# Experts' tokens gathered as rows from rows split in two float32r parts, then transposed; the experts' weight ring of ten slots in three places

## The chip, the cores and the metric

The kernel runs on one core of one Trainium2 chip. The metric is the device time of one execution in microseconds (us), the median of the runs shown. TensorE multiplies and transposes, VectorE and ScalarE work on rows and move results out of the accumulators (PSUM), GpSimd does small arithmetic on SBUF, and SyncE's queue starts nearly all the loads.

## The reference

Two networks run one after the other on 512 tokens of 1024 numbers, in float32. Only the end of the first matters here, a layer of 16 experts in which each expert picks its 64 best tokens:

```
aff = softmax(h @ w_router)                  # 512 x 16
g, idx = top_k(aff transposed, 64)           # each of 16 experts picks 64 tokens
xs = h[idx]                                  # 16 x 64 x 1024
y = (silu(xs @ w_gate) * (xs @ w_up)) @ w_down * g
out = sum of y at the tokens that it came from
```

h is the normalised row times (1 + scale) plus shift. After this layer the first network's final norm follows, and then the second network, whose first part is a feed-forward layer.

## The kernel before, in words

Everything is written with a tile framework: pools of tiles in SBUF and PSUM, instructions in program order, and a scheduler that puts them in order on each engine's queue by their readiness in its own model. The order on each queue is fixed when the kernel is built.

All weights come through one object, W. Its pieces (chunks of up to 1 MB, 128 partitions x 2048 numbers) are loaded in the order in which they are used, by SyncE's queue, into slots of a ring. Before the experts' stage the ring has NR = 4 slots (ring 0). For the experts a second ring of NR2 = 5 slots (ring 1) is opened, and piece number n goes to ring 0 if n mod 9 is under 4, otherwise to ring 1, so that both together are a ring of nine. A slot is used again when the matmuls that read it are done. The second network's weights go through ring 0 alone.

Experts are worked on in pairs, q = 0 to 7, 64 tokens each, so 128 columns. A pair has 24 pieces: 8 each of gate, up and down. The stage is this loop:

```
xs, hx = gather(0), None
for q in range(NE // 2 + 1):
    if q < NE // 2:
        outs = gate_up(xs)
        if q + 1 < NE // 2:
            xs = gather(q + 1)
    if q > 0:
        done = down(q - 1, hx)
    if q < NE // 2:
        hx = hidden(q, outs)
    if q > 0:
        scatter(*done)
```

So the gather of the next pair stands beside gate and up of this one, and one turn of the loop is called a round below. A gather makes a one-hot matrix oh (token rows x 128 slots) on VectorE (L855), and multiplies the normalised rows h2f with it so that the result has features as rows, 128 slots as columns (L864): 2 groups x 4 blocks x 4 row tiles, in float32, of which the profile shows two instructions for each matmul. VectorE applies scale and shift on the way to xs (L867, L868). The expert matmuls are in both() at L885, in float32, the two experts of a pair side by side in 64 columns each. hidden() transposes the hidden rows (L906) and copies them (L907); scatter() is at L932 and L934.

h2f comes from normed(t) at L744, ScalarE, for each of four row tiles, during the projection before the stage. The xs tiles use, one after the other, the two large tiles bigh and bigl (16 KB a partition each), which hold matrix operands before and after this stage. The stage begins with the ranking of the tokens on VectorE (L821, L822), for which an exponential (L792) and a transpose come first; the first gather follows it. After the loop come the final norm, the norm of the second network (L277) and its first weights, which are split in two float32r parts, whi on ScalarE (L156) and wlo on VectorE (L157). float32r is float32 read at reduced precision by TensorE; a number split into a rounded part and the rest needs a matmul for each part.

Of the kernel before, what the change touches and what calls it, by code (L numbers as in the profile page):

```python
# [9 lines left out]
F32 = mybir.dt.float32  # L10
F32R = mybir.dt.float32r
BF = mybir.dt.bfloat16
I32 = mybir.dt.int32
AF = mybir.ActivationFunctionType
OP = mybir.AluOpType
# [3 lines left out]
P = 128  # L19
D = 1024  # L20
S = 512
T = S // P
K = D // P
# [6 lines left out]
CAP = 64  # L30
# [16 lines left out]
MAGIC = 12582912.0  # L47

NR = 4
NR2 = 5  # L50
NU = 4
BANDW = 640
RW = "tile"
# [41 lines left out]
def f(ap):  # L95
    return ap.bitcast(F32)


class Weights:
# [25 lines left out]
    def pump(self):  # L125
        while self.dma_at < len(self.chunks):
            srcs, shape, ring = self.chunks[self.dma_at]
            if not self.room.get(ring):
                return
            self.room[ring] -= 1  # L130
            n = int(np.prod(shape[1:]))
            t = self.pools[ring].tile([P, 2048], F32, name="wraw", tag="wraw")
            v = t[:, :n]
            if len(shape) == 3:
                v = v.rearrange("p (a b) -> p a b", b=shape[2])
            for p0, p1, ap in srcs:
                self.nc.sync.dma_start(out=v[p0:p1], in_=ap)
            self.tiles[self.dma_at] = v
            self.dma_at += 1
# [46 lines left out]
def tile_net(ctx, tc, I, out):  # L186
    nc = tc.nc
    V, A, PE, G = nc.vector, nc.scalar, nc.tensor, nc.gpsimd
# [3 lines left out]
    big = ctx.enter_context(tc.tile_pool(name="big", bufs=2))  # L192
# [9 lines left out]
    W = Weights(nc, raw, NR)  # L202

    def psA():
        return psh[0].tile([P, 1024], F32, name="pA", tag="pA")

    def psB():
        return psh[0].tile([P, 512], F32, name="pB", tag="pB")

    def psC():  # L210
        return psh[0].tile([P, 512], F32, name="pC", tag="pC")
# [3 lines left out]
    def psBC():  # L215
        turn[0] ^= 1
        return psB() if turn[0] else psC()

    cst = const.tile([P, C_KEEP], F32, name="cst")
    X = const.tile([P, T, D], F32, name="X")  # L220
# [9 lines left out]
    ident = cst[:, C_ID:C_ID + P]  # L230
# [112 lines left out]
    for k0 in (4, 6, 0, 2):  # L343
# [5 lines left out]
        c = W.chunk(srcs, (P, 2, D))  # L349
# [9 lines left out]
                W.unit(c, lambda v, u=u: v[:, u:u + 1])  # L359

    nth = [0]

    def plan_pair(w, q):

        for c0 in range(0, D, 256):
            for e in (2 * q, 2 * q + 1):
                c = W.chunk([(0, P, w[e][c0:c0 + 256].rearrange("(p j) n -> p (j n)", j=2))], (P, 2048),
                            ring=int(nth[0] % (NR + NR2) >= NR))
                nth[0] += 1
                W.unit(c, lambda v: v.rearrange("p (j n) -> p j n", j=2), raw=2)  # L370

    for q in range(NE // 2 + 1):
        if q < NE // 2:
            plan_pair(wg, q)
            plan_pair(wu, q)
        if q > 0:
            plan_pair(wd, q - 1)
# [16 lines left out]
    c = W.chunk([(0, P, I["pool_w_2"][0].rearrange("g (k p) n -> p (g k) n", p=P))], (P, 8, 256))  # L394
# [39 lines left out]
    qpool = rowp.enter_context(tc.tile_pool(name="rowp", reuse_waits=RW, bufs=1, side="right"))  # L434
# [60 lines left out]
    for s in range(2):  # L495
# [5 lines left out]
                        in_=I["w_router"][0].rearrange("(c p j) n -> p c (j n)", p=P, j=2))  # L501
# [47 lines left out]
    for b in range(6):  # L549
        xs, t = nxt  # L550
# [7 lines left out]
    for b0 in (0, 2, 4):  # L558
# [11 lines left out]
        for s in range(2):  # L570
            p = psBC()
            for b in range(2):
                for g in range(KV):
# [3 lines left out]
                                             in_=p.rearrange("p (g t) -> p g t", g=KV))  # L577
# [4 lines left out]
    for u in range(4):  # L582
        w = W.next()
        for kk in range(2):
            k = u * 2 + kk
# [3 lines left out]
    for t in range(T):  # L589
# [5 lines left out]
        for g in range(2):  # L595
            p = psA()
# [35 lines left out]
    def twos(row):  # L632

        return row.rearrange("r (c p j) -> r c j p", p=P, j=2)
# [87 lines left out]
        values(n, g, *cur)  # L722


    h2f = qpool.tile([P, T, D], F32, name="h2f", tag="q")
    h2f = [h2f[:, t] for t in range(T)]
    for t in range(T):
        nc.gpsimd.dma_start(out=X[:, t], in_=x_in[t * P:(t + 1) * P])
    accs = []
    for t in range(T):  # L730
        if t < 2:
            a = psA()
# [8 lines left out]
    rs = []  # L741

    def normed(t):
        A.activation(h2f[t], X[:, t], AF.Copy, scale=rs[t])  # L744

    lgp, xts = [], []
    lgs = att.tile([P, T, NE], F32, name="lgs", bufs=1)
# [26 lines left out]
    for t in range(T):  # L774
        for j in range(3):
            z = K - 3 + j
            project_out(t, z, order[z], ws[j])
        for dh in range(2):
            tmp = att.tile([P, 512], F32, name="tmp", tag=("PTh", "PTl")[dh], bufs=2)
            c_ = slice(dh * 512, (dh + 1) * 512)  # L780
            V.tensor_mul(tmp, accs[2 * t + dh], gt1[:, c_])
            (G if dh and t + 1 < T else V).tensor_tensor(out=X[:, t, c_], in0=X[:, t, c_], in1=tmp, op=OP.add)
        if t > 0:
            turned_x(t - 1)
        rs.append(row_rstd(att, X[:, t], D))
        if t > 0:
            logits(t - 1)
            normed(t - 1)
    turned_x(T - 1)
    logits(T - 1)  # L790
    V.tensor_sub(aff, lgs, mx[:, :, None].to_broadcast([P, T, NE]))
    A.activation(aff, aff, AF.Exp)  # L792
    normed(T - 1)
    V.reduce_sum(mx, aff, axis=AX.X)
    V.reciprocal(mx, mx)
# [8 lines left out]
    moe = ExitStack()  # L804
    W.open_ring(1, moe.enter_context(tc.tile_pool(name="raw2", reuse_waits=RW, bufs=NR2)), NR2)
    mp = moe.enter_context(tc.tile_pool(name="moep", reuse_waits=RW, bufs=1))
    slot = mp.tile([P, T, NE], F32, name="slot")
    slotT = mp.tile([NE, S], F32R, name="slotT")
    gcol = mp.tile([P, NE // 2], F32, name="gcol")
    pick = mp.tile([NE, NE // 2, P], F32R, name="pick")  # L810
    V.tensor_copy(pick.rearrange("n q (e c) -> n (q e) c", c=64), ident[:NE, :NE, None].to_broadcast([NE, NE, 64]))
    st = ExitStack()
    rp = st.enter_context(tc.tile_pool(name="rp", reuse_waits=RW, bufs=1))
    p = psB()
# [9 lines left out]
    p = psC()  # L824
# [9 lines left out]
    p = psB()  # L834
# [7 lines left out]
    p = psC()  # L842
# [5 lines left out]
    ex = moe.enter_context(tc.tile_pool(name="ex", reuse_waits=RW, bufs=2))  # L848
    iota = cst[:, C_IOTA:C_IOTA + 64]

    def gather(q):

        oh = ex.tile([P, T, 2, CAP], F32, name="oh", tag="oh", bufs=1)
        for t in range(T):
            V.tensor_tensor(oh[:, t], iota[:, None, :].to_broadcast([P, 2, CAP]),  # L855
                            slot[:, t, 2 * q:2 * q + 2, None].to_broadcast([P, 2, CAP]), op=OP.is_equal)
        ohf = oh.rearrange("p t e c -> p t (e c)")
        xs = big.tile([P, K * S], F32, name="xs", tag=("bigh", "bigl")[q % 2], bufs=1)[:, :K * P]
        xs = xs.rearrange("p (k c) -> p k c", k=K)
        for g in range(2):  # L860
            p = psC()
            for a in range(4):
                for t in range(T):
                    PE.matmul(p[:, a * P:(a + 1) * P], twos(h2f[t])[:, 2 * g + a // 2, a % 2], ohf[:, t],  # L864
                              start=t == 0, stop=t == T - 1)
            k_ = slice(4 * g, 4 * g + 4)
            V.tensor_mul(xs[:, k_], p.rearrange("p (k c) -> p k c", k=4), sc2[:, k_, None].to_broadcast([P, 4, P]))  # L867
            V.tensor_add(xs[:, k_], xs[:, k_], sh2[:, k_, None].to_broadcast([P, 4, P]))  # L868
        pg = psC()
        for t in range(T):  # L870
            PE.matmul(pg[:, 0:NE], ohf[:, t], aff[:, t], start=t == 0, stop=t == T - 1)
        for j in range(2):
            V.tensor_copy(gcol[j * 64:j * 64 + 64, q:q + 1], pg[j * 64:j * 64 + 64, 2 * q + j:2 * q + j + 1])
        return xs
# [52 lines left out]
    def scatter(Se, ys):  # L927
        for t in range(T):
            for dh in range(2):
# [4 lines left out]
                V.tensor_add(X[:, t, c_], p, X[:, t, c_])  # L934
# [13 lines that stand above are left out]
# [495 lines left out]
```

## Time and profile before

| | |
|---|---|
| median of 3 runs | 2734.22 us (2734.2 to 2737.8) |
| profiled execution, its own time | 2732.16 us |
| its span in the trace | 2730.0 us |
| mean granted TensorE clock | 0.983 of full speed |
| TensorE matmul busy | 2599.0 us, 95% |
| VectorE, ScalarE, GpSimd busy | 39%, 27%, 3% |
| bytes loaded | 411.94 MB, mean 151 GB/s |

The span is what lies between the first and the last instruction of the profiled execution. Busy times of matmuls are modelled at their ends, so neighbouring matmuls overlap in the rows; the distance between starts says what one costs in a row of them. A DMA share of 1.00 means that all 16 DMA engines were busy.

### The profile page before, as it was taken

To read this page: it belongs to the slowest core of one execution; us is meant where nothing else is said; L and a number is where in the kernel's file an instruction comes from. 1 tells how busy PE (TensorE), PEld (TensorE's weight loads), DVE (VectorE), ACT (ScalarE), POOL (GpSimd) and SP (SyncE) were. 2 spreads that over 40 slices of the span, in tenths; PEclk is the share of its full clock that TensorE was granted. 3 is DMA by queue.
4 is the path that set the end of the run, shared out by engine and by line. 5 is a ranking of instruction groups with operands and counts; after the bars stand their busy time and mean duration, and the time that the engine had idled before them with its cause. 6 is when DMAs were issued, how large, how long until landed. Compare 5 with 4: busy or idle time off the path is not lost.

```text
span 2730.0 us, 29692 instructions
## 1 busy us (share of the span) xinstructions
PE 2599.0 (95%) x12362; PEld 1908.7 (70%) x12362; DVE 1067.1 (39%) x1661; ACT 734.1 (27%) x1268; POOL 78.9 (3%) x138
## 2 busy tenths in 40 slices
PE   5988979999999899999999999999999999999999
PEld 3864755444443688887877777887878777788887
DVE  4646441222221533335533334333334566533332
ACT  4324310000000422223322223222223555422221
POOL 1000000000000100000000000000001100000000
PEclk8989979999999899999999999999999999999999
DMA  8226139999999422322222332322222212122321
GB/s 298 66 105 215 55 159 394 384 389 394 390 392 407 159 95 76 116 89 92 84 102 75 103 100 84 107 95 85 85 92 69 66 57 78 62 93 77 101 89 58
DMA packets 179254, 411.94 MB, mean 151 GB/s; under 512 B 7364, under 2 KB 120544, under 8 KB 151472
## 3 DMA queue, kind: packets, MB, share of 16 engines
q1 hardware_dynamic: 176928, 403.73, 40.5%
q0 software_dynamic: 1184, 2.97, 0.4%
q10 hardware_dynamic: 1008, 3.34, 0.3%
q8 instruction: 97, 1.59, 0.2%
q14 instruction: 37, 0.30, 0.0%
HBM read 407.92 MB, written 2.10 MB: 150 GB/s over the span
## 4 chain that ended last, share of the span: by engine, by line
PE 59%; issue 29%; DVE 3%; ACT 3%; DMA 3%; POOL 1%; ACTq 0%; POOLq 0%; DVEq 0%
PE pA L885 9%; PE pA L242 7%; PE pA L243 7%; PE pA L244 7%; PE pB L885 4%; PE pC L864 3%; PE pC L243 2%; PE pC L242 2%; PE pC L244 2%; PE pB L244 2%; PE pB L243 2%; PE pB L242 2%; DMA wraw<-in_w_ada_dram 1%; PE ms L1314 1%; PE pC L932 1%
## 5 line engine op out<-in xcount | busy, mean ns | idle before, releaser
L156 ACT CAST whi<-wraw 128x1024 fp32r<-128x1024 f32 (+2 forms) x334 | 336.2, 1011 | 1108.1 <-PE pA L243 681.9
L243 PE MATMUL pA<-xTl,whi 128*128 128x512 f32 (+1 forms) x1536 | 578.6, 377 | 1.6 <-DVE xTl L251 1.6
L157 DVE TENSOR_TENSOR wlo<-wraw,whi 128x1024 fp32r<-128x1024 f32 (+2 forms) x334 | 392.2, 1177 | 480.6 <-ACT whi L156 473.2
L244 PE MATMUL pA<-xTh,wlo 128*128 128x512 f32 (+1 forms) x1536 | 578.5, 377 | 0.0
L242 PE MATMUL pA<-xTh,whi 128*128 128x512 f32 (+1 forms) x1536 | 574.8, 382 | 1.7 <-ACT xTh L250 1.3
L242 PEld LDWEIGHTS pA<-xTh,whi 128*128 128x128 f32 x1536 | 290.1, 189 | 77.4 <-ACT sl L969 22.1
L244 PEld LDWEIGHTS pA<-xTh,wlo 128*128 128x128 f32 x1536 | 290.3, 189 | 56.7
L243 PEld LDWEIGHTS pA<-xTl,whi 128*128 128x128 f32 x1536 | 290.4, 189 | 55.3 <-DVE xTl L251 2.1
L885 PE MATMUL pA<-wraw,xs 128*64 128x512 f32 x1024 | 256.7, 598 | 1.5 <-DMA wraw<-in_w_up_dram 1.3
L971 DVE TENSOR_TENSOR sl<-pA,sl 128x512 f32<-128x512 f32 x88 | 60.8, 691 | 427.4 <-PE pA L244 427.3
L885 PEld LDWEIGHTS pA<-wraw,xs 128*64 128x64 f32 x1024 | 73.9, 136 | 136.5 <-issue 128.7
L243 PE MATMUL pC<-wlo,hh 128*128 128x512 f32 x352 | 138.5, 393 | 0.0
L244 PE MATMUL pC<-whi,hl 128*128 128x512 f32 x352 | 138.5, 393 | 0.0
L242 PE MATMUL pC<-whi,hh 128*128 128x512 f32 x352 | 138.4, 393 | 0.0
L242 PE MATMUL pB<-whi,hh 128*128 128x512 f32 x352 | 138.3, 393 | 0.0
L243 PE MATMUL pB<-wlo,hh 128*128 128x512 f32 x352 | 138.3, 393 | 0.0
L244 PE MATMUL pB<-whi,hl 128*128 128x512 f32 x352 | 138.1, 392 | 0.0
L885 PE MATMUL pB<-wraw,hx 128*64 128x512 f32 x512 | 130.7, 596 | 1.6 <-DMA wraw<-in_w_down_dram 1.6
L885 PEld LDWEIGHTS pB<-wraw,hx 128*64 128x64 f32 x512 | 45.9, 136 | 73.3 <-issue 67.2
L864 PEld LDWEIGHTS pC<-oh,h2f 128*128 128x128 f32 x512 | 65.3, 202 | 30.1 <-issue 29.2
L242 PEld LDWEIGHTS pB<-whi,hh 128*128 128x128 f32 x352 | 66.1, 188 | 15.6 <-DVE X L1020 0.7
L244 PEld LDWEIGHTS pB<-whi,hl 128*128 128x128 f32 x352 | 66.1, 188 | 14.9
(474 smaller groups left out, 3201.3 us busy)
## 6 DMA issues: line engine op xcount, KB each, us to landing
wraw<-in_w_gate_dram SPq DMA_DIRECT2D x64, 1024.0 KB, 11.7
wraw<-in_w_up_dram SPq DMA_DIRECT2D x64, 1024.0 KB, 9.0
wraw<-in_w_down_dram SPq DMA_DIRECT2D x64, 1024.0 KB, 7.7
wraw<-in_ffn_w_gate_dram SPq DMA_DIRECT2D x40, 1024.0 KB, 5.2
wraw<-in_ffn_w_up_dram SPq DMA_DIRECT2D x40, 1024.0 KB, 5.2
wraw<-in_ffn_w_down_dram SPq DMA_DIRECT2D x32, 1024.0 KB, 5.0
wraw<-in_w_ada_dram SPq DMA_DIRECT2D x24, 1024.0 KB, 9.5
wraw<-in_ffn_w_down_dram SPq DMA_DIRECT2D x16, 768.0 KB, 4.4
```

The lines of the kernel that those rows point to most:

```text
L156: self.nc.scalar.copy(out=hi, in_=src)
L157: self.nc.vector.tensor_sub(lo, src, f(hi))
L242: PE.matmul(o, a[0], b[0], start=first, stop=False)
L243: PE.matmul(o, a[0], b[1], start=False, stop=False)
L244: PE.matmul(o, a[1], b[0], start=False, stop=last)
L864: PE.matmul(p[:, a * P:(a + 1) * P], twos(h2f[t])[:, 2 * g + a // 2, a % 2], ohf[:, t], start=t == 0, stop=t == T - 1)
L885: PE.matmul(outs[dh][r], x[:, k, r], ws[e][:, j, dh * 512:(dh + 1) * 512], start=k == 0, stop=k == K - 1)
L932: PE.matmul(p, Se[:, t * P:(t + 1) * P], ys[dh][s], start=s == 0, stop=s == 1)
L971: V.tensor_mul(sl, a[:, 512:1024], sl)
L1314: PE.matmul(p[:, :nn], q[a][:, c_], k[b][:, :nn], start=first, stop=False)
```

## The change

The gather is turned round. The normalised rows are kept in two float32r parts: h2h, the rounded row, written by normed(), and h2l, the rest, made after the projection by a ScalarE copy of the normalised row into a tile "got" and a GpSimd subtraction, for each of four row tiles. A gather now multiplies the one-hot matrix, now float32r, from the left: 128 slots as rows, 512 features as columns, two halves, four row tiles, two parts, 16 matmuls. ScalarE copies each half to got (one buffer), and eight transposes bring it to features as rows. Scale and shift follow on VectorE as before.

The ring for the experts has ten slots in three places: ring 0 with four, ring 1 with three, and ring 2 with three, which lie in the two large tiles bigh and bigl, now one tile "wide" each for the whole stage. Both xs buffers lie in the first half of the first of them.

```diff
 NR = 4
-NR2 = 5
+NR2 = 3
+NR3 = 3
...
-            t = self.pools[ring].tile([P, 2048], F32, name="wraw", tag="wraw")
+            if isinstance(self.pools[ring], list):
+                t = self.pools[ring].pop(0)
+                self.pools[ring].append(t)
+            else:
+                t = self.pools[ring].tile([P, 2048], F32, name="wraw", tag="wraw")
...
+    NRS = NR + NR2 + NR3
...
-                            ring=int(nth[0] % (NR + NR2) >= NR))
+                            ring=(NR <= nth[0] % NRS) + (NR + NR2 <= nth[0] % NRS))
...
-    h2f = qpool.tile([P, T, D], F32, name="h2f", tag="q")
-    h2f = [h2f[:, t] for t in range(T)]
+    h2h = qpool.tile([P, T, D], F32R, name="h2h", tag="q")
...
     def normed(t):
-        A.activation(h2f[t], X[:, t], AF.Copy, scale=rs[t])
+        A.activation(h2h[:, t], X[:, t], AF.Copy, scale=rs[t])
...
+    h2l = mp.tile([P, T, D], F32R, name="h2l")
+    for t in range(T):
+        got = mp.tile([P, D], F32, name="got", tag="got")
+        A.activation(got, X[:, t], AF.Copy, scale=rs[t])
+        G.tensor_tensor(out=h2l[:, t], in0=got, in1=f(h2h[:, t]), op=OP.subtract)
+
+    wide = [big.tile([P, K * S], F32, name="wide" + z, tag="big" + z, bufs=1) for z in "hl"]
+    xsb = [wide[0][:, z * D:(z + 1) * D].rearrange("p (k c) -> p k c", k=K) for z in range(2)]
+    W.open_ring(2, [wide[0][:, 2048:4096], wide[1][:, 0:2048], wide[1][:, 2048:4096]], NR3)
...
-        oh = ex.tile([P, T, 2, CAP], F32, name="oh", tag="oh", bufs=1)
+        oh = ex.tile([P, T, 2, CAP], F32R, name="oh", tag="oh", bufs=1)
...
-        ohf = oh.rearrange("p t e c -> p t (e c)")
-        xs = big.tile([P, K * S], F32, name="xs", tag=("bigh", "bigl")[q % 2], bufs=1)[:, :K * P]
-        xs = xs.rearrange("p (k c) -> p k c", k=K)
+        ohr = oh.rearrange("p t e c -> p t (e c)")
+        ohf = f(ohr)
+        got = mp.tile([P, D], F32, name="got", tag="got")
+        for dh in range(2):
+            c_ = slice(dh * 512, (dh + 1) * 512)
+            p = psC()
+            for t in range(T):
+                for z, h in enumerate((h2h, h2l)):
+                    PE.matmul(p, ohr[:, t], h[:, t, c_], start=t + z == 0, stop=t + z == T)
+            A.copy(out=got[:, c_], in_=p)
+        xs = xsb[q % 2]
         for g in range(2):
             p = psC()
             for a in range(4):
-                for t in range(T):
-                    PE.matmul(p[:, a * P:(a + 1) * P], twos(h2f[t])[:, 2 * g + a // 2, a % 2], ohf[:, t],
-                              start=t == 0, stop=t == T - 1)
+                PE.transpose(p[:, a * P:(a + 1) * P], twos(got)[:, 2 * g + a // 2, a % 2], ident)
```

## Rows read from the trace of the kernel before

**Rows 1.** The page: engines' busy time, and load rate in 40 equal slices.

```profile
PE 2599.0 (95%) x12362; PEld 1908.7 (70%) x12362; DVE 1067.1 (39%) x1661; ACT 734.1 (27%) x1268; POOL 78.9 (3%) x138
...
GB/s 298 66 105 215 55 159 394 384 389 394 390 392 407 159 95 76 116 89 92 84 102 75 103 100 84 107 95 85 85 92 69 66 57 78 62 93 77 101 89 58
```

**Rows 2.** Windows by stage: length, engines' busy us, PE clock, DMA share, GB/s.

```profile
391.00:820.00 429.00, 422.92 (x1956) 185.70 (x1957) 93.49 (x172) 19.13 (x33) 0.00 (x0) 1.00 0.95 387
820.00:892.00 72.00, 67.63 (x272) 23.49 (x272) 13.56 (x21) 3.49 (x6) 0.00 (x0) 1.00 0.96 393
```

**Rows 3.** Windows by round, one of five that are alike.

```profile
498.20:562.90 64.70, 63.69 (x291) 27.65 (x289) 14.55 (x26) 2.91 (x5) 0.00 (x0) 1.00 0.94 383
```

**Rows 4.** Windows of 10 us: the stage's first, and one inside a round.

```profile
390.00:400.00 10.00, 10.00 (x54) 4.17 (x54) 2.50 (x8) 0.00 (x0) 0.00 (x0) 1.00 0.41 153
...
540.00:550.00 10.00, 10.00 (x50) 4.06 (x48) 0.00 (x0) 0.00 (x0) 0.00 (x0) 1.00 1.01 419
```

**Rows 5.** Issues of loads; what ended idle time before L885 (us, times).

```profile
wraw<-in_w_gate_dram SPq DMA_DIRECT2D x64, 1024.0 KB, 11.7
...
  DMA wraw<-in_w_down_dram: 6.2, 8
```

**Rows 6.** One gather in a round: the chain (start, us), then the timeline.

```profile
498.27 1.38 PE pC L864 x10
...
504.90 2.55 PE pC L864 x20
...
512.70 2.79 PE pC L864 x22
...
503.16 0.74 PE L864 MATMUL pC<-oh,h2f 128*128 128x128 f32 x4
503.83 1.07 PE L885 MATMUL pA<-wraw,xs 128*64 128x512 f32 x2
```

**Rows 7.** Nearest operations: timeline, first and last of 50; the chain; line groups.

```profile
319.63 0.39 PE L242 MATMUL pC<-whi,mixTh 128*128 128x512 f32 x1
...
330.84 0.39 PE L243 MATMUL pA<-wlo,mixTh 128*128 128x512 f32 x1
...
472.36 1.16 PE pC L906 x8
...
L907 ACT COPY hx<-pC 128x512 f32<-128x512 f32 x8 | 4.7, 586 | 152.8 <-PE pC L906 128.2 <-issue 24.5
```

**Rows 8.** Timeline of the way into the stage, all engines (start, us).

```profile
344.44 1.66 POOL L782 TENSOR_TENSOR X<-X,tmp 128x512 f32<-128x512 f32 x1 [4.38 <-DVE tmp L781]
...
354.90 1.15 ACT L744 ACTIVATE h2f<-X,rstd 128x1024 f32<-128x1024 f32 x1 [0.47 <-POOL rstd L258]
...
363.07 0.26 ACT L792 ACTIVATE aff<-aff 128x64 f32<-128x64 f32 x1 [7.02 <-DVE aff L791]
...
380.75 9.65 PE L864 MATMUL pC<-oh,h2f 128*128 128x128 f32 x64
...
387.39 0.69 DVE L868 TENSOR_TENSOR xs<-xs,sh 128x512 f32<-128x512 f32 x1
...
391.13 4.08 PE L885 MATMUL pA<-wraw,xs 128*64 128x512 f32 x18
...
391.59 0.69 DVE L868 TENSOR_TENSOR xs<-xs,sh 128x512 f32<-128x512 f32 x1
```

**Rows 9.** The way out: timelines of SyncE's queue and VectorE; GpSimd's powers.

```profile
868.34 0.38 SPq L137 DMA_DIRECT2D wraw<-in_ffn_w_gate_dram  x1
888.00 0.38 SPq L137 DMA_DIRECT2D wraw<-in_ffn_w_up_dram  x1
...
900.48 1.21 DVE L157 TENSOR_TENSOR wlo<-wraw,whi 128x1024 fp32r<-128x1024 f32 x1
901.62 1.28 DVE L277 SCALAR_TENSOR_TENSOR hrow<-X,rstd,gain 128x1024 f32<-128x1024 f32 x1
...
L258 POOL TENSOR_TENSOR rstd<-ms,mhalf x8: 548/548/1469, 896.4 to 921.0; 128x1 f32<-128x1 f32 x8
```

## The prediction

> **What bounds the kernel now.** I read the page first: TensorE is busy for 95% of the span, and one stretch of it is also the stretch of highest load rate, the slices at 384 to 407 GB/s [rows 1]. That stretch is the experts' stage, the only place that the diff touches, so the rest of the span was left alone. The windows by stage put the experts' body at 391 to 820 us and its tail at 820 to 892 us [rows 2]. In the body TensorE is busy for 422.9 of 429 us, while the loads run at 387 GB/s. One window per pair of experts then shows what a round is: 64.7 us, PE busy 63.7 of it, DMA share 0.94, 383 GB/s; there are five such rounds, alike within 0.1 us and 10 GB/s [rows 3].
>
> Which of the two is the bound? A stretch inside a round shows the loads at 419 GB/s with a share of 1.01 and PE at 10.00 of 10 us [rows 4]. So the loads can go faster than the round's mean beside a full TensorE. A round loads 24 pieces of 1024 KB, 25.17 MB [rows 5]; at 419 GB/s that is 60.1 us. The round of 64.7 us is thus TensorE's, and the loads sit 4.6 us below it. In the tail, where nothing is gathered, it is the other way round: the expert matmuls' idle time before a weight load has 6.2 us that end with the landing of a piece of the down weights [rows 5]. The reader is to see two limits 7% apart: what is taken from TensorE counts until the loads are reached.
>
> The Trainium skill, page "DMA: Bandwidth & Descriptors", section "Where 436 GB/s comes from", says that for HBM to SBUF transfers the HBM side binds, at about 358 GB/s. By that a round could not be shorter than 25.17 / 0.358 = 70.3 us, an estimate from the page, and the change could win nothing. This trace disagrees: whole rounds run at 383 GB/s, and stretches at 419 [rows 3, 4].
>
> **The change, part by part.** *Gather on TensorE.* Now a gather is 64 matrix instructions at L864. In a regular round the chain shows 52 of them in three pieces of 1.38, 2.55 and 2.79 us; the other 12 stand in three pieces of 4, each 503.83 - 503.16 = 0.67 us [rows 6]. Together 8.73 us. After the change there are 16 float32r matmuls 512 columns wide (2 halves x 4 row tiles x 2 parts) and 8 transposes. Float32r matmuls of that width stand in a row before this stage, 50 of them from 319.63 to 330.84, so 0.229 us each [rows 7]: 3.66 us. Eight transposes of the same shape, those of the hidden rows, take 1.16 us [rows 7]. Together 4.82 us, so 3.9 us less in each round. Seven gathers lie inside rounds (1 to 7): -27.3 us. A round would be 60.8 us, still just above the loads' 60.1.
>
> *Hand-offs that are new.* Each gather now goes matmul, ScalarE copy, transpose, VectorE, where it went matmul, VectorE. Two copies of 128x512 at 0.59 us [rows 7] stand between. ScalarE is nearly idle there, and the gate matmuls that now stand among the gather's pieces can run meanwhile. If they all do, the cost is nothing; if both copies stand bare in PE's queue with about 0.7 us more each for the hand-overs, it is 2.6 us a round. The order of PE's queue after the change is not to be read from this trace; it now mixes gather and gate finely [rows 6], so I take 0.5 us a round, +3.5 us, bounds 0 and +18.
>
> *Low parts of the rows.* Four ScalarE copies (1.15 us, as the one at L744) and four GpSimd subtractions of 128x1024; a GpSimd addition of half that size takes 1.66 us [rows 8], so 3.3 us each. With the single buffer "got" they alternate: 4 x 4.45 = 17.8 us. The last high part is ready at 354.90 + 1.15 = 356.05, and the first gather matmul is at 380.75 [rows 8]: 24.7 us of room, held open by the ranking of tokens on VectorE, so I cost it at nothing. With that cover gone it would be the whole 17.8 us. Behind the copies on ScalarE's queue is the exponential at 363.07 [rows 8], with which the ranking begins: if a copy that waits for GpSimd is put before it, the ranking starts up to one subtraction, 3.3 us, later for each copy ahead.
>
> For the subtractions there is a rule against this change: the Trainium skill, page "SBUF — State Buffer", section "SBUF: two separate sides", says that a VectorE operation with two SBUF inputs and a GpSimd operation that reads SBUF block each other for a whole instruction. The trace agrees: among eight equal GpSimd powers of 0.548 us one took 1.469 us [rows 9], and it ran beside the VectorE step at 901.62, which has two such inputs. By the rule a ranking whose steps had two inputs would wait for the subtractions, 13 us; its steps have one large input, the tensor work.
>
> *First gather.* It stands bare: 10.4 us from the first gather matmul at 380.75 to the first gate matmul at 391.13 [rows 8], the clock being low at first (64 instructions in 9.65 us here against 8.73). Afterwards: 8 matmuls at half speed 3.7, 8 partly so 2.7, copy with hand-over 0.8, the first four transposes 0.6, two VectorE steps of 0.69 us [rows 8] 1.4: 9.2 us, so -1 us (0 to -3).
>
> *Ring of ten.* One more piece, 2.5 us of loading at 419 GB/s, is in place when the rounds start, and the queue can run one piece further ahead. This counts where TensorE waits for loads, in the tail: -2 us (0 to -2.5).
>
> *Which slots the next network finds.* With nine slots, piece 191 is the third in its turn, and only one of the four slots of the first ring is free before the last experts: the first load of the next network goes at 868.34, the second only at 888.00 [rows 9]. With ten, 191 is the second in its turn, so two slots are free and the second load goes some 20 us earlier. What it holds up today is the split at 900.48 on VectorE, ahead of the normalised row at 901.62 [rows 9]: -1 us (0 to -3).
>
> The xs buffers move into one tile, still two of them, so no wait is added there. DMA issues stay the same in number and order.
>
> **The sum.** -27.3 + 3.5 - 1 - 2 - 1 = -27.8 us, against the profiled execution's own 2732.2 us: 2704.4. Its median stands 2.0 us higher, at 2734.2, so 2706 us against that. The loads give a floor of their own: in the body they move 387 x 429 = 166.0 MB, 396 us at 419 GB/s, so 33 us are idle; in the first 10 us, before the first refill, the share is 0.41 [rows 4], so 6 of these stay. That leaves 27 us, 2.5 for the tenth piece, 3 and 3 for start and end at their best: -36 us, 2698. So the two limits nearly coincide, and TensorE's stalls, not its sum, decide the size.
>
> **The rivals.** *Bare hand-offs.* The copies and the ScalarE queue cost all they can: +18 instead of +3.5, and up to 3 at the ranking: about 2722. For it: at the scatter PE waits for ScalarE and VectorE in every round, which is what fills the 1.0 us that a round's PE is not busy [rows 3]. Against it: gate matmuls of another bank are there to fill.
>
> *The loads are the bound already.* If the round's 383 GB/s were all that the loads give in the long run, 24 pieces would take 65.7 us, the round itself, and the time would stay at 2732 to 2734, or 2731 with the tenth piece. The skill's rule above points there. Against it: 419 GB/s over ten microseconds beside a busy PE [rows 4].
>
> *The low parts come late.* The subtractions and the ranking hold each other: +13 us, 2719. Against it: the room of 24.7 us; the ranking reads one tensor at a time.
>
> *Slower: loads into the wide tiles wait for readers of the other parts.* Three slots of the ring and both xs now share two tiles. If a load into one part waited for matmuls that read another, one load per ten would wait for up to a gate-and-up block, 128 x 4.08 / 18 = 29 us [rows 8], with every later load behind it on the one queue, while the ring covers 25 us. At half a block for each of eight rounds that is +116 us, less the 28: about 2820. It decides from 3.5 us of such waiting in a round on. Against it: today the gate matmuls start at 391.13 while the other half of the same xs tile is still being written at 391.59 [rows 8], so parts of a tile are told apart.
>
> **How the numbers follow.** Forecast 0.62, around 2706 (2698 to 2713). Bare hand-offs 0.15, late low parts 0.08, both inside the range's upper part; loads already the bound 0.06; slower 0.07; 0.02 for a gain beyond the floor. The range of 2698 to 2722 leaves out 0.15 to 0.2. What a measurement of this kernel can tell from no change is about 0.2%, 5.5 us. Faster: 0.62 + 0.15 + 0.08 + 0.02 = 0.87; same 0.06; slower 0.07.
>
> **What would show it.** Right: rounds of 60 to 61.5 us at 409 GB/s or more; a gather of 16 + 8 instructions in about 4.8 us; a DMA share near 1.00; the first gate matmul near 390; the next network's second load before 870. Wrong: rounds over 63 us with PE idle behind a copy; gather matmuls that wait for GpSimd; a load into a wide tile that waits while its own slot's readers are done.

## The result, and the profile after

The changed kernel takes 2702.31 us (median of 4 runs, 2700.42 to 2703.63) against 2734.21 us: a ratio of 0.9881, interval 0.9869 to 0.9893. Its profiled execution took 2703.63 us with a span of 2701.6 us, 28.4 us less than the span before.

The page answers [rows 1]: matmul busy time is 30 us less, and the stage's slices now show 414 to 419 GB/s.

```profile
PE 2568.8 (95%) x12042; PEld 1879.9 (70%) x12042; DVE 1066.7 (39%) x1661; ACT 748.4 (28%) x1288; POOL 88.5 (3%) x142
...
GB/s 301 67 86 221 71 164 419 414 418 418 416 417 342 124 94 90 105 86 102 74 94 90 106 86 86 108 80 102 78 101 73 63 57 63 63 94 78 108 83 59
```

The windows by stage and by round answer [rows 2, 3]. The body's DMA share went from 0.95 to 1.00. A round is 60.36 us instead of 64.70, at 417 GB/s; five are alike within 0.05 us.

```profile
391.00:820.00 429.00, 421.05 (x1794) 166.34 (x1791) 94.07 (x169) 28.45 (x49) 0.00 (x0) 1.00 1.00 414
820.00:862.00 42.00, 39.01 (x145) 13.84 (x144) 10.72 (x17) 2.44 (x4) 0.00 (x0) 1.00 0.97 386
539.77:600.13 60.36, 59.35 (x250) 23.60 (x250) 14.59 (x28) 4.08 (x7) 0.00 (x0) 1.00 1.01 417
```

The chain through one round's gather answers [rows 6] (start, us, what). The gather proper stands in five pieces, L879 and L885, from one start to the next 1.36 + 0.67 + 2.51 + 0.68 + 0.43 = 5.65 us (5.54 by the starts in the timeline, where the last is 0.34). Between them two groups of 16 expert matmul instructions are cut into 14 and 2.

```profile
489.62 1.35 PE pC L879 x5
490.98 3.58 PE pA L905 x14
494.55 0.66 PE pC L879 x2
495.22 1.00 PE pA L905 x2
496.22 2.28 PE pC L879 x9
498.50 0.23 PE pC L885 x2
498.73 3.58 PE pA L905 x14
502.31 0.68 PE pC L885 x4
502.99 1.00 PE pA L905 x2
503.99 0.43 PE pC L885 x2
504.42 0.80 PE pC L891 x8
```

The way into the stage answers [rows 8]. The low parts begin on ScalarE at 363.68, behind the exponential, not at 356; the last subtraction ends at 378.09. From the first gather matmul to the first gate matmul it is 388.91 - 381.06 = 7.85 us instead of 10.4.

```profile
363.68 1.13 ACT L819 ACTIVATE got<-X,rstd 128x1024 f32<-128x1024 f32 x1
...
364.89 2.40 POOL L820 TENSOR_TENSOR h2l<-got,h2h 128x1024 fp32r<-128x1024 f32 x1 [8.77 <-ACT got L819]
...
375.75 2.34 POOL L820 TENSOR_TENSOR h2l<-got,h2h 128x1024 fp32r<-128x1024 f32 x1 [1.26 <-ACT got L819]
...
378.27 0.41 DVE L837 TENSOR_SCALAR work<-work 16x512 f32<-16x512 f32 x1
...
381.06 0.77 PE L879 MATMUL pC<-h2h,oh 128*128 128x512 f32 x1
...
388.91 0.65 PE L905 MATMUL pA<-wraw,wideh 128*64 128x512 f32 x2 [0.48 <-DVE wideh L888]
```

The way out answers [rows 9], first SyncE's queue, then VectorE. The row yt, the last result of the last down matmuls, stood at 890.58 before and stands at 860.36 now: 30.2 us earlier. The next network's second load goes at 839.48 instead of 888.00. From yt to the first normalised row, hrow, it is 11.03 us, and it was 11.04. What follows the last yt, code that the change does not touch, took 2701.6 - 860.36 = 1841.2 us, and 2730.0 - 890.58 = 1839.4 before; over all the runs below it lies between 1837.7 and 1843.0. So the stage gained 30.2 us and the span 28.4, and whole times scatter by some microseconds for reasons outside the stage.

```profile
839.48 11.46 SPq L142 DMA_DIRECT2D wraw<-in_ffn_w_up_dram  x1
```

```profile
860.36 1.61 DVE L940 SCALAR_TENSOR_TENSOR yt<-pB,gcol,gt 128x512 f32<-128x512 f32 x2 [8.83 <-PE pB L905]
...
870.26 1.22 DVE L162 TENSOR_TENSOR wlo<-wraw,whi 128x1024 fp32r<-128x1024 f32 x1
871.39 1.28 DVE L282 SCALAR_TENSOR_TENSOR hrow<-X,rstd,gain 128x1024 f32<-128x1024 f32 x1
```

### The profile page after: what moved, and what is told of

Same layout as the page of the kernel before. It is cut to its first block, busy times and chain, and to the rows that moved or that the text cites. A ratio compares the mean times of both kernels' runs of the same rounds, so it can differ in the third digit from the quotient of the medians.

```text
span 2701.6 us, 29081 instructions
## 1 busy us (share of the span) xinstructions
PE 2568.8 (95%) x12042; PEld 1879.9 (70%) x12042; DVE 1066.7 (39%) x1661; ACT 748.4 (28%) x1288; POOL 88.5 (3%) x142
## 4 chain that ended last, share of the span: by engine, by line
PE 58%; issue 30%; DVE 4%; ACT 3%; DMA 3%; POOL 1%; ACTq 0%; POOLq 0%; DVEq 0%; SPq 0%
PE pA L905 8%; PE pA L247 7%; PE pA L248 7%; PE pA L249 7%; PE pB L905 4%; PE pC L248 2%; PE pC L247 2%; PE pC L249 2%; PE pB L249 2%; PE pB L247 2%; PE pB L248 2%; DMA wraw<-in_w_ada_dram 1%; PE pC L879 1%; PE pC L952 1%; PE ms L1334 1%
## 5 line engine op out<-in xcount | busy, mean ns | idle before, releaser
L905 PE MATMUL pA<-wraw,wideh 128*64 128x512 f32 x736 | 202.6, 598 | 1.9 <-DMA wraw<-in_w_up_dram 1.4
L905 PEld LDWEIGHTS pA<-wraw,wideh 128*64 128x64 f32 x736 | 58.3, 136 | 93.2 <-issue 88.2
L905 PE MATMUL pB<-wraw,hx 128*64 128x512 f32 x344 | 101.0, 597 | 1.1 <-DMA wraw<-in_w_down_dram 1.1
L247 PEld LDWEIGHTS pC<-whi,hh 128*128 128x128 f32 x352 | 66.1, 188 | 15.0
L248 PEld LDWEIGHTS pB<-wlo,hh 128*128 128x128 f32 x352 | 66.1, 188 | 14.8
## 6 DMA issues: line engine op xcount, KB each, us to landing
wraw<-in_w_gate_dram SPq DMA_DIRECT2D x47, 1024.0 KB, 13.3
```

Source lines behind the costliest of these rows:

```text
L247: PE.matmul(o, a[0], b[0], start=first, stop=False)
L248: PE.matmul(o, a[0], b[1], start=False, stop=False)
L905: PE.matmul(outs[dh][r], x[:, k, r], ws[e][:, j, dh * 512:(dh + 1) * 512], start=k == 0, stop=k == K - 1)
```

## The experiments

Each time is a median beside a run of the kernel before on the same chip. Two points of the traces serve as a ruler: the first refill (the first load that SyncE's queue issues in the stage, when the first slot comes free), and the last yt. Between them 192 pieces less the ring's must be loaded: 183 with nine slots, 182 with ten, 181 with eleven. At the 420 GB/s that the best whole rounds show, a piece is 1.0486 MB / 420 GB/s = 2.497 us. The last column is what the stage takes from the first refill to the last yt beyond that. "Round" is the median distance of the yt rows of neighbouring rounds. The two points before, and the first of them after (the second stands above):

```profile
394.81 10.63 SPq L137 DMA_DIRECT2D wraw<-in_w_up_dram  x7
890.58 1.61 DVE L920 SCALAR_TENSOR_TENSOR yt<-pB,gcol,gt 128x512 f32<-128x512 f32 x2 [8.83 <-PE pB L885]
```

```profile
392.59 7.69 SPq L142 DMA_DIRECT2D wraw<-in_w_up_dram  x6
```

| kernel | time, us | ratio, interval | round | first refill | last yt | beyond the loads |
|---|---|---|---|---|---|---|
| before, ring of 9 | 2734.21 | 1 | 64.71 | 394.81 | 890.58 | 38.8 |
| old gather, ring of 10 | 2728.91 | 0.9982 [0.9973, 0.9991] | 64.71 | 394.82 | 887.96 | 38.7 |
| old gather in one block, 9 | 2720.66 | 0.9951 [0.9939, 0.9964] | 61.18 | 402.12 | 874.84 | 15.8 |
| new gather, ring of 9 | 2707.02 | 0.9899 [0.9886, 0.9913] | 60.34 | 393.23 | 863.60 | 13.4 |
| changed kernel, 10 | 2702.31 | 0.9881 [0.9869, 0.9893] | 60.33 | 392.59 | 860.36 | 13.3 |
| changed, ring of 11 | 2701.24 | 0.9884 [0.9870, 0.9897] | 60.34 | 392.78 | 858.38 | 13.6 |
| low parts added twice, 10 | 2723.00 | 0.9963 [0.9950, 0.9975] | 63.65 | 395.21 | 881.60 | 31.9 |
| high parts only, 10 | 2697.68 | 0.9866 [0.9851, 0.9881] | 59.84 | 393.79 | 858.89 | 10.6 |
| low parts made twice, 10 | 2708.07 | 0.9909 [0.9894, 0.9925] | 60.34 | 398.87 | 866.05 | 12.7 |
| half the bytes loaded, 10 | 2665.09 | 0.9751 [0.9738, 0.9765] | 56.24 | 390.04 | 825.07 | |
| new gather in one block, 10 | 2705.74 | 0.9901 [0.9884, 0.9917] | 59.84 | 397.79 | 863.33 | 11.1 |
| the same, 11 | 2702.25 | 0.9887 [0.9872, 0.9902] | 59.93 | 398.01 | 860.96 | 11.0 |
| in one block from the third gather, 10 | 2702.45 | 0.9879 [0.9865, 0.9894] | 59.84 | 393.04 | 858.84 | 11.3 |
| the same, 11 | 2700.34 | 0.9876 [0.9859, 0.9892] | 59.84 | 392.62 | 855.94 | 11.4 |

**The two halves of the change apart.** The new gather with a ring of nine:

```diff
-NR3 = 3
+NR3 = 2
-    W.open_ring(2, [wide[0][:, 2048:4096], wide[1][:, 0:2048], wide[1][:, 2048:4096]], NR3)
+    W.open_ring(2, [wide[0][:, 2048:4096], wide[1][:, 0:2048]], NR3)
```

> The gather stays turned round, the ring has nine slots again (ring 2 has two). If TensorE sets the rounds and the loads lie just under it, the tenth slot matters at the two ends alone: one load of 2.5 us less is in place at the start, and the queue runs out a little more often; following the pieces one by one through the slots at 2.5 us a load gives +3 to +5 us against the changed kernel, rounds of 60.4 us as they are. Rival (the ten slots carry the gain): +15 us or more, rounds back over 62 us.

And the old gather with the ring of ten in three places:

```diff
-NR2 = 5
+NR2 = 3
+NR3 = 3
...
-        xs = big.tile([P, K * S], F32, name="xs", tag=("bigh", "bigl")[q % 2], bufs=1)[:, :K * P]
-        xs = xs.rearrange("p (k c) -> p k c", k=K)
+        xs = xsb[q % 2]
```

> The gather of before (64 float32 instructions, 8.7 us), the ring of ten in three places. If the gather carries the gain: rounds stay at 64.7 us, and only the tenth slot's 2.5 us of loading counts, -2 to -3 us against the kernel before, 2731. Rival (the ten slots carry the gain): -15 us or more.

In the stage both came out as expected. From refill to yt the four corners are 495.77 (old, nine), 493.14 (old, ten), 470.37 (new, nine) and 467.77 (new, ten): the ring is worth 2.6 us with either gather, the gather 25.4 us with either ring, and 1.6 to 2.2 us more before the refill. Nothing is left for an interaction. In whole times the new gather with nine slots is 4.7 us above the changed kernel (3 to 5 expected), and the old gather with ten is 5.6 us under its kernel before, where 2 to 3 were expected; the stage shows 2.6 of these, the rest does not come from it.

**More and less work in the gather.** The low parts of the rows left out of the gather, and the low parts added twice:

```diff
-                for z, h in enumerate((h2h, h2l)):
-                    PE.matmul(p, ohr[:, t], h[:, t, c_], start=t + z == 0, stop=t + z == T)
+                PE.matmul(p, ohr[:, t], h2h[:, t, c_], start=t == 0, stop=t == T - 1)
```

> The gather multiplies the high part alone: 8 float32r matmuls of 0.23 us, 1.8 us, are left out of each gather, and with them the low part of the rows. If the loads (60.1 us a round at 419 GB/s) lie just under TensorE's 60.4 us, only 0.3 us a round can be won, 0 to -3 us against the changed kernel, and TensorE begins to wait for pieces. Rival (TensorE alone sets the pace, the loads are far off): -1.8 us a round, -13 us.

```diff
-                for z, h in enumerate((h2h, h2l)):
-                    PE.matmul(p, ohr[:, t], h[:, t, c_], start=t + z == 0, stop=t + z == T)
+                for z, h in enumerate((h2h, h2l, h2l)):
+                    PE.matmul(p, ohr[:, t], h[:, t, c_], start=t + z == 0, stop=t + z == T + 1)
```

> The low part is added twice: 8 more float32r matmuls, 1.8 us of TensorE, in each gather. If TensorE sets the rounds: rounds of 62.2 us, +10 to +13 us against the changed kernel. Rival (the loads set the rounds, TensorE has slack): less than +3 us, rounds within 0.5 us of 60.4.

The windows of one round, first with the low parts left out, then with them added twice:

```profile
535.09:594.93 59.84, 58.06 (x242) 22.17 (x241) 14.39 (x27) 4.08 (x7) 0.00 (x0) 1.00 1.01 419
```

```profile
548.74:612.41 63.67, 62.45 (x258) 24.99 (x257) 14.47 (x27) 4.08 (x7) 0.00 (x0) 1.00 0.97 397
```

Eight matmuls less, 1.83 us of work, shorten the round by 0.5 us and bring the loads to 419 GB/s, share 1.01: here the loads bind, and the stage ends only 1.5 us earlier. Its median is 4.6 us lower, beyond the 0 to 3 expected; from refill to yt it is 2.7 us. In this run the idle time of TensorE's weight loads that ends with a landing is 21.7 us from 391 to 820 us; it is 3.4 us in the changed kernel. Eight more lengthen the round by 3.3 us, nearly twice their work, and the stage by 21.2 us where 10 to 13 were expected. The miss is instructive: the gather's pieces are 2.46 us longer, since beside the 1.83 us of work the last four transposes now wait for ScalarE's copy, and a third group of 16 expert matmul instructions is cut (14 of it, then the small products of L891, then the rest). So a gather has a price beyond its instructions.

**The cut itself.** The old gather, put into TensorE's queue in one block:

```diff
-            for a in range(4):
-                for t in range(T):
-                    PE.matmul(p[:, a * P:(a + 1) * P], twos(h2f[t])[:, 2 * g + a // 2, a % 2], ohf[:, t],
-                              start=t == 0, stop=t == T - 1)
+            with tc.high_priority(offset=200):
+                for a in range(4):
+                    for t in range(T):
+                        PE.matmul(p[:, a * P:(a + 1) * P], twos(h2f[t])[:, 2 * g + a // 2, a % 2], ohf[:, t],
+                                  start=t == 0, stop=t == T - 1)
```

> The kernel before, with its 32 float32 gather matmuls of a round (64 instructions) put into one uninterrupted block of TensorE's queue, and not in six pieces between gate matmuls; nothing else differs. Theory: a change between the expert matmuls, which use 64 columns, and matmuls that use all 128 costs TensorE about half a us (a group of 16 expert instructions takes 3.43 us in one piece in the changed kernel's rounds, 4.58 us as 14 and 2 with a piece of gather between). Three groups are split in a round of the kernel before, so rounds of about 61 us and -15 to -22 us against it. Rival (the order is free, only the instructions count): rounds of 64.7 us, 0 to -3 us.

```profile
547.18:608.36 61.18, 59.71 (x290) 26.80 (x289) 14.36 (x26) 2.91 (x5) 0.00 (x0) 1.00 1.00 412
```

The window is one of its rounds: 3.5 us less than [rows 3] with the same 64 instructions and the same arithmetic. They now stand in one piece of 7.73 us (8.73 in six pieces before), and the three groups that were cut 14 + 2 [rows 6 show one such 2] are whole. TensorE's busy time falls by 63.69 - 59.71 = 3.98 us, 1.00 in the gather's own pieces and 2.98 in the expert instructions, all from order alone. It is a gain that the changed kernel does not have in full, since it still cuts two groups. The round of 61.18 us is the one expected; the time is not, 12.4 us less instead of 15 to 22, for the first refill is 7.3 us later (402.12), and TensorE's weight loads already wait for pieces (12.7 us in the body). What a cut costs is read from the changed kernel's chain, 490.98 to 494.55 and 495.22 to 496.22: 4.57 us for 16 expert instructions; in one piece, in the timeline of the new gather in one block, the same 16 take 628.17 - 624.68 = 3.49 us:

```profile
624.68 3.65 PE L907 MATMUL pA<-wraw,wideh 128*64 128x512 f32 x16
628.17 0.59 PE L907 MATMUL pA<-wideh 128*64 128x512 f32 x1
```

So 1.1 us for a cut. The timeline of the changed kernel shows what it consists of, in a round where the two experts' weights lie in tiles of different names:

```profile
553.43 0.59 PE L905 MATMUL pA<-wideh 128*64 128x512 f32 x1
553.44 0.59 PE L905 MATMUL pA<-wraw,wideh 128*64 128x512 f32 x1
553.86 1.02 PE L905 MATMUL pA<-wideh 128*64 128x512 f32 x2
554.82 0.50 PE L879 MATMUL pC<-h2l,oh 128*128 128x512 f32 x1
...
555.48 1.07 PE L905 MATMUL pA<-widel,wideh 128*64 128x512 f32 x2
556.48 0.50 PE L879 MATMUL pC<-h2l,oh 128*128 128x512 f32 x1
```

The expert instructions run in twos, one of each expert, 64 columns each: two start within 0.01 us, the next 0.43 us later, so 16 are eight steps. This cut goes through two such twos. Two instructions of one expert run alone from 553.86, 0.96 us, and the other expert's two alone from 555.48, 1.00 us, where the four side by side would take two steps, 0.86 us. Of the 1.10 us more, 0.86 is two further steps of 0.43, and 0.24 is left for the edges of the pieces. A cut between twos shows the edges alone: four instructions between scatter matmuls take 1.01 us instead of 0.86.

```profile
485.62 1.01 PE pA L905 x4
```

The expectation's reason, half a us for each change between 64 and 128 columns, was thus right in its sum only. The Trainium skill, page "TensorEngine Tiling (Array Packing)", section "Key Properties", says that a change of tiling mode, not just of the tile, drains TensorE; the trace agrees in kind, but what a cut's changes of width can cost here is the 0.24 us at the edges, not the 1.1.

**The low parts.** Each subtraction made twice:

```diff
         G.tensor_tensor(out=h2l[:, t], in0=got, in1=f(h2h[:, t]), op=OP.subtract)
+        G.tensor_tensor(out=h2l[:, t], in0=got, in1=f(h2h[:, t]), op=OP.subtract)
```

> Each of the four GpSimd subtractions that make the low parts is done twice, 9.4 us more. In the changed kernel the last of them ends at 378.1 us, and the low parts are needed from 381.6 us on, so 3.5 to 5 us are covered and the first gate matmul comes 4 to 6 us later: +4 to +6 us against the changed kernel. Rival (the room is the 24.7 us that the prediction took): 0.

As expected: the time is 5.8 us more, the last yt 5.7 us later. The first gate matmul is 6.3 us later (395.19), 1.0 of which lies before the first copy (364.70 against 363.68) and is not the edit's. The timeline, all engines, shows two mechanisms:

```profile
378.00 2.34 POOL L820 TENSOR_TENSOR h2l<-got,h2h 128x1024 fp32r<-128x1024 f32 x1 [1.26 <-ACT got L819]
...
379.29 1.32 DVE L838 TENSOR_SCALAR work<-work 16x512 f32<-16x512 f32 x1
...
381.70 1.17 DVE L855 TENSOR_SCALAR self<-self 128x64 f32<-128x64 f32 x1
...
386.52 2.35 POOL L821 TENSOR_TENSOR h2l<-got,h2h 128x1024 fp32r<-128x1024 f32 x1
...
388.92 0.51 PE L880 MATMUL pC<-h2l,oh 128*128 128x512 f32 x1 [1.87 <-POOL h2l L821]
```

The eighth gather matmul waits at 388.92 for the last subtraction, which is plain lateness. The two VectorE steps L838 and L855 (names of this kernel) take 1.32 and 1.17 us beside a subtraction, and 0.41 and 0.20 us in the changed kernel, where the last subtraction ends at 378.09 and the first of them starts at 378.27. The ranking steps before them, MAX8 and MATCH_REPLACE8, keep their 0.68 and 0.66 us beside subtractions. The Trainium skill, page "SBUF — State Buffer", section "Who interferes with whom", says that a VectorE tensor_scalar can use the port pair that it shares with GpSimd and that whoever comes later then waits for the whole instruction; the trace agrees for these two steps. The changed kernel has 0.18 us to spare at that place.

**The loads taken away.** Of each piece after the first ten only half the bytes are loaded:

```diff
-                self.nc.sync.dma_start(out=v[p0:p1], in_=ap)
+                if self.half[0] + 10 <= self.dma_at < self.half[1]:
+                    self.nc.sync.dma_start(out=v[p0:p1, 0:1024], in_=ap[:, 0:1024])
+                else:
+                    self.nc.sync.dma_start(out=v[p0:p1], in_=ap)
```

> Of each expert piece after the first ten, the second half of the bytes is not loaded, so that the slot keeps what it held; all else is as in the changed kernel. If TensorE sets the rounds: still 60.4 us each, and only the waits at the two ends go, -3 to -6 us against the changed kernel. Rival (the loads set the rounds): rounds under 59 us, -10 us or more.

```profile
528.11:584.39 56.28, 56.28 (x250) 22.58 (x249) 14.30 (x27) 4.08 (x7) 0.00 (x0) 1.00 0.66 222
```

The half that is not loaded keeps old numbers, and the ten slots are held as ten fixed tiles. The expectation missed: 37 us less instead of 3 to 6, with rounds under 59 us, which it had put down to loads that set the rounds. The run does not show that by itself, because TensorE's queue was also built in another order, with the gather's sixteen products in one block. But its round is TensorE's own, 56.28 us busy of 56.28: that is what TensorE needs in a good order, and it is 3.6 us under the 59.9 us that 24 pieces take at 420 GB/s.

**The loads' floor.** That calls for the new gather in one block with the loads whole:

```diff
+            with tc.high_priority(offset=200):
                 for t in range(T):
                     for z, h in enumerate((h2h, h2l)):
                         PE.matmul(p, ohr[:, t], h[:, t, c_], start=t + z == 0, stop=t + z == T)
...
+                with tc.high_priority(offset=200):
                     PE.transpose(p[:, a * P:(a + 1) * P], twos(got)[:, 2 * g + a // 2, a % 2], ident)
```

> The changed kernel, with the gather's products and transposes put in TensorE's queue in one piece, so that fewer groups of expert products are cut in two. Theory (TensorE's round of 60.4 us stands only just above the loads' 60.0 us): TensorE alone would need 56 to 58 us (56.3 in the run that loads half as much), but the loads hold the round at 59.8 to 60.1 us. 0 to 3 us less than the changed kernel, and TensorE is now seen to wait for pieces of the weights. Rival (the loads are no floor): rounds under 58.5 us, 12 us or more gained.

```profile
539.53:599.36 59.83, 58.20 (x250) 23.17 (x249) 14.37 (x26) 3.98 (x7) 0.00 (x0) 1.00 1.01 419
```

The round is 59.83 us at a DMA share of 1.01: the floor, not TensorE's 56.3. The waits of TensorE's weight loads in the five rounds from 479.4 to 780 us (total us, times, longest) now show them waiting for pieces, 13.8 us together:

```profile
PEld pB L907 <- DMA wraw<-in_w_down_dram: 8.9, 9, 1.5
...
PEld pB L907 <- DMA widel<-in_w_down_dram: 2.5, 3, 1.4
PEld pB L907 <- DMA wideh<-in_w_down_dram: 2.4, 2, 1.4
```

In the changed kernel there is none in those rounds; over the body there is one line:

```profile
PEld pA L905 <- DMA wraw<-in_w_up_dram: 3.4, 3, 2.3
```

(One of the five rounds, the third, took 61.40 us with the loads at 420 GB/s all the while; why it is 1.5 us longer was not settled.) The rounds came as expected and the time did not: it is not under the changed kernel. The ruler says why. The second pair's gather now stands ahead of most of the first gate matmuls, so the first slot comes free 5.2 us later (397.79 against 392.59), and all else follows at the loads' pace:

```profile
397.79 9.35 SPq L142 DMA_DIRECT2D wraw<-in_w_up_dram  x6
```

```profile
863.33 1.61 DVE L942 SCALAR_TENSOR_TENSOR yt<-pB,gcol,gt 128x512 f32<-128x512 f32 x2 [8.84 <-PE pB L907]
```

863.33 - 397.79 = 465.54 us, 2.2 us less than the changed kernel's 467.77, but from a later start. With a ring of eleven:

```diff
-NR2 = 3
+NR2 = 4
```

> As the kernel before it in this call, with one more place in the weight ring (eleven). Theory: where loads are the bound, what counts is how much of the weights lies ready when the stage starts; one more piece of 1 MB is 2.5 us of loading, so 3 to 6 us less than the changed kernel, about 2697 to 2699 us. Rival (the ring's size no longer matters, TensorE is the bound): no difference to the kernel before it.

2702.25 us, 3.5 us under the kernel before it and not the 2697 to 2699 expected. One piece less is worth 2.6 us from refill to yt, so the ring's size still matters; the absolute time missed for the same late start. The ring of eleven in the changed kernel without a block:

> One more slot (ring 1 has four), eleven in all. If loads and TensorE are both at their limit and the stage ends with the loads, one more piece loaded ahead is worth its 2.5 us: -2 to -3 us against the changed kernel. Rival (TensorE alone): 0.

Its yt is 2.0 us earlier, its median 1.1 us lower where 2 to 3 were expected; the measurement does not tell such differences apart.

**The version that the ruler points to.** In one block only from the third pair's gather on, so that the first refill stays early:

```diff
-            with tc.high_priority(offset=200):
+            with (tc.high_priority(offset=200) if q > 1 else ExitStack()):
```

The same condition also reached two places in the code behind the stage, where q is 8 and it changes nothing.

> As the kernel with the gather in one piece, but only from the third pair's gather on; the first two stand in the queue as in the changed kernel. Theory (in that kernel the second pair's gather stood ahead of the first expert products, so the first refill went out at 397.8 us instead of 392.6, and from there the loads alone set the end): the stage ends 465.5 us after the first refill, that is at 858 us where the changed kernel has 860.4; time 2699 to 2701 us, 4 to 6 us under the kernel with all gathers in one piece. Rival (one piece costs something of its own, as got and its copies stand bare): 2704 to 2706 us as before.

> The same with a ring of eleven. Theory: one piece of 1 MB fewer to load after the start, 2.5 us: stage end at 855 to 856.5 us, time 2696 to 2699 us, which would be under the changed kernel by 3 to 6 us. Rival: no different from the kernel before it.

```profile
392.62 7.19 SPq L142 DMA_DIRECT2D wraw<-in_w_up_dram  x5
```

```profile
855.94 1.61 DVE L942 SCALAR_TENSOR_TENSOR yt<-pB,gcol,gt 128x512 f32<-128x512 f32 x2 [8.83 <-PE pB L907]
```

These two rows are the first refill and the last yt of the second of them, 463.32 us apart. Both yt came where the ruler put them (858.84 for 858, 855.94 for 855 to 856.5), 1.5 and 4.4 us before the changed kernel's, so no cost of the block itself shows. The medians, 2702.45 and 2700.34 us, are 1 to 2 us above the expected ranges; the intervals of their ratios overlap that of the changed kernel. That the second is faster than the changed kernel is shown for the stage, not for the whole time.

## Why the prediction was right, step by step

The forecast was 2706 us in a range of its own of 2698 to 2713; measured 2702.31. Between the profiled executions the sum was -27.8 us, and the measured difference is 2703.63 - 2732.16 = -28.5. The bound was named rightly: TensorE's round with the loads' floor just below it. That the sum fits to 0.7 us is in part luck. The stage gained 30.2 us where the terms inside it add up to 26.8: 25.4 by the gather and 2.6 by the ring from refill to yt, and 2.2 before the refill. The untouched rest took 1.8 us longer. And several terms were off and cancelled.

- **The gather, -3.9 us a round.** A round lost 4.34 us, not 3.9, and by another account. The 24 instructions take 5.54 us, not 4.82: the 16 matmuls 4.20 instead of 3.66, because the first and the last of a piece cost up to 0.34 us where those between cost 0.23, and the transposes 1.34 instead of 1.16. So the arithmetic gave 3.19 us. The other 1.15 came from the queue's order: two expert groups are cut instead of three. The step took a row's price for one in a block and left out what the places in the queue cost, with the old gather and the new.
- **Hand-offs, +3.5 (0 to 18).** Nearly nothing, the lower bound: other gate matmuls stand between the pieces, and the waits of the transposes' weight loads for the copy are 1.2 us in the whole body.
- **Low parts, nothing.** Right in size, wrong in its cover. The copies begin 7.6 us later than planned (363.68, behind the exponential on ScalarE), which left 17.4 us up to the first gather matmul at 381.06, not 24.7; a subtraction took 2.34 us, not 3.3, so the work took 14.4 us. The 3.3 was twice the 1.66 us of an addition of half the size at 344.44 [rows 8], and that row was no price of GpSimd alone: VectorE's addition with two SBUF inputs had begun 0.16 us earlier.

```profile
344.28 0.68 DVE L782 TENSOR_TENSOR X<-X,tmp 128x512 f32<-128x512 f32 x1
```

If GpSimd waited until its end at 344.96, as the blocking that the prediction names would have it, 344.44 + 1.66 - 344.96 = 1.14 us are left for the addition, about half of 2.34. All three such additions of the trace stand so, and no run parts the two, so this stays argued. Twice the subtractions cost 5.7 us. The ranking was not held up, as argued, though two steps at its end would have been.
- **First gather, -1 (0 to -3).** 7.85 us instead of 10.4, so -2.5: five of its sixteen matmuls stand 0.42 to 0.57 us apart and the last ten 0.23; the prediction had eight slow and eight partly so. It was mis-sized, inside its bounds.
- **Ring of ten, -2 (0 to -2.5).** -2.6 us with either gather, one piece at 2.5 us.
- **Next network's start, -1 (0 to -3).** This step failed. The second load does go 48 us earlier, 18 of them against the last yt, but wlo stands where it stood: before and after it begins right behind VectorE's additions to X, and yt to hrow takes 11.03 us against 11.04. The new gather with nine slots, where that load goes at 861.01, also takes 11.03 us. VectorE's queue held it, not the load.

The loads' floor was used rightly. Of the 33 us that the prediction read as idle time of the loads, 38.8 - 11.1 = 27.7 us are what the ruler shows beyond the best kernels, and the changed kernel took all but 2.2 of them.

The rivals. *Bare hand-offs*: not seen. *Loads already the bound at 383 GB/s*: refuted, rounds run at 417 and, where TensorE leaves room, at 420 GB/s. (383 was the lowest of the five rounds before, 383 to 392; at 383, 24 pieces take 65.7 us, longer than the 64.7 us round.) *Low parts late*: not seen, true with twice the work. *Loads into the wide tiles wait for other parts' readers*: refuted; with the old gather the ring of nine, with no slot in a wide tile, and the ring of ten, with three, differ by one piece's 2.6 us in favour of ten, and the changed kernel's rounds run at a DMA share of 1.01.

## What to carry to other kernels

When two limits lie 7% apart, taking work from one is worth only the distance, and the next gain is somewhere else: here in when the first slot comes free and how many pieces lie ready. Count for an instruction stream not only its instructions but where it cuts another stream: the same 64 instructions in one block saved 3.5 us of a 64.7 us round. Above all do not cut between two matmuls that would run side by side, for apart they take two steps instead of one. Before a row serves as a price, look at what ran beside it. And when a stage is bound by loads, set a ruler from the first refill to the last result before reading any busy time.

## What was not expected of the hardware

- A cut in a run of paired 64-column matmuls by 128-column ones costs 1.1 us (4.57 against 3.49 us for 16 instructions), of which 0.86 us is that four instructions lose the partner beside which they ran, and 0.24 us the edges.
- The loads keep 420 GB/s over whole rounds of 59.8 us beside a TensorE at a granted clock of 1.00; the trace before showed it for ten microseconds [rows 4].
- A GpSimd subtraction of 128x1024 took 2.34 us beside VectorE steps with one large input. The addition of half the size took 1.66 us [rows 8] beside a VectorE addition with two SBUF inputs, so the two do not give a price by size.
- Two VectorE steps of 0.41 and 0.20 us took 1.32 and 1.17 us beside a GpSimd subtraction.
